# One split of V per chunk, low parts in a pool of their own, a later row load and 52 gather pairs beside the routing

## The chip, the cores and the metric

The kernel runs on one core of a Trainium2 chip. The metric is the time of one execution on the device in microseconds (us). A profiled execution gives the trace from which all rows below come.

## The reference, cut to what matters

The program is a block of attention, gated recurrence and a retrieval layer (PEER), followed by a second block of two layers. The change lies in the retrieval layer, which works on 512 tokens of width 1024 with 16384 experts, stored as two tables U and V of 16384 rows:

```python
q = (t @ wq)                        # 8 heads, two halves each
s1, i1 = top_k(s[:, :, 0], 16); s2, i2 = top_k(s[:, :, 1], 16)
cand = s1[..., :, None] + s2[..., None, :]
top, pos = top_k(cand, 16); idx = take(cidx, pos)   # 16 experts a head
g = softmax(top)
a = gelu(einsum('tpkd,td->tpk', u[idx], t))
out = einsum('tpk,tpkd->td', g * a, v[idx])
```

So each token uses 8 x 16 = 128 of the 16384 experts, with weight g times gelu of its product with a row of U, and sums rows of V.

## The kernel before, in words

**Two ways for the tokens.** The 512 tokens are four tiles of 128. Tiles 1 to 3 (384 tokens, TD) are computed densely: the product with all of U, gelu, times a weight that is zero for experts not chosen, then the product with all of V. Tile 0 goes by gathers: for each of its 128 choices an indirect DMA on POOL fetches one row of U (later of V) per token, 128 rows of 4 KB, and VectorE multiplies and sums it (`gathered`, L1142 to L1169). There are 256 such loads. They are stepped in pairs of two loads (one `next(gather)` is a pair), with a ring of five buffers and a lead of four loads.

**Stage U** (`ahead`, `rows_u`, `hidden`). Chunk e of 128 holds 128 experts. U is loaded by SP, split into a high and a low part (ACT L1349, DVE L1350) because a product is made of three products of parts, 24 matmuls a chunk. The result after gelu (L1364) is written to the DRAM tensor `Ad` from ACT's queue (L1374). Beside it the routing runs on DVE (`topk` for each tile, `spread`, which makes the dense weights `W` and writes them to the DRAM tensor `Wd`). `weave` emits three generators by virtual clocks: the chunks of U at 2.66 each, the routing by the values that it yields, and the gather pairs at GATHER[phase] each, where the phase is the number of the routing's turn. Turn 0 is `topk` of tile 0, turn 1 `topk` of tile 1, turns 2 and 3 are a `topk` and a `spread`, turn 4 is the last `spread`. Summed from the code, one `topk` yields 47.6 and one `spread` 46.4. The pairs that didn't fit stay for stage V as `gather_left`, out of 130.

**Stage V** (L1047 to L1083). For each chunk `operands` loads the 384 gelu values back (`act`, SP, L1384) and 512 KB of V (`w`, SP, L1386), multiplies `act` with the weights `Wr` (DVE, L1390), splits V and the product into `vh`, `vl`, `sh`, `sl` (ACT L1391 and L1392, DVE L1393 and L1394), in two of eight chunks has no load of weights and in the other six loads a sixth of the next group's `Wr` (SP, L1406), and at its end splits V a second time by `split` (ACT L134, DVE L136) under the same tile names. The operands that `products` takes are those of the second split. `products` makes 18 matmuls of 512 columns a chunk, four chunks behind (OPS_LAG). The order on PE, DVE and ACT is the order written in this loop. The gather pairs that are left are spread evenly over the first 120 chunks.

**Memory around it.** Pools are a stack from the left and one from the right. `h2`, the moving rows of U (32 KB of a partition), is the first on the right and is shut after U's last chunk. Then `pm` opens on the right and holds all operands of V. A tile waits only for the tiles that lay on its bytes. On the left `ar` opens where `pa` (the `act` tiles of stage U) lay, for one row of gates `gt2r`, loaded by SP (L371) and used after V (L1096). After V, `pt` opens on the right where the operands lay.

Of the kernel before, what the change touches and what calls it, by code (L numbers as in the profile page):

```python
# [8 lines left out]
FR = mybir.dt.float32r  # L9
# [13 lines left out]
TD = S - T0  # L23
# [5 lines left out]
VBUFS = 6  # L29
# [2 lines left out]
WT = 16  # L32
GBUFS = 5
GAHEAD = 4
GATHER = (13.0, 13.0, 9.0, 6.0, 4.5)
OPS_LAG = 4
TAIL = 2
STATE = 3.0
# [14 lines left out]
def run(gen):  # L53
    while True:
        try:
            next(gen)
        except StopIteration as e:
            return e.value


def steps(gen, n):
    for _ in range(n):
        yield next(gen)


def weave(*gens):

    at = [[0.0, i, g] for i, g in enumerate(gens)]
    while at:
        cur = min(at, key=lambda x: (x[0], x[1]))  # L70
        try:
            cur[0] += next(cur[2])
        except StopIteration:
            at.remove(cur)
# [18 lines left out]
class Net:  # L93
# [931 lines left out]
    def peer(self):  # L1025
        nc, p = self.nc, self.p
        hh, hl = self.h2
        mv = ([hh[:, k] for k in range(KC)], [hl[:, k] for k in range(KC)])
        first = self.proj_first(self.ws, mv, lambda i: self.normed_half(i, [(hh, hl, self.a2)], 1e-6, self.sh2))
        self.finish = None  # L1030
        for name in ("wo", "st", "hca", "y", "pn"):
            self.shut(name)
        mk = self.pool("mk")
        self.mk = mk.tile([128, 2, 2, C], F32, name="mk")
        self.mv = mk.tile([128, 2, 2, C], F32, name="mv")
        self.open_stream()
        self.Wd = self.tc.dram_tile([TD // WT, 128, 128, WT], F32, name="Wd")
        self.Ad = self.tc.dram_tile([128, 128, TD], F32, name="Ad")
        pg = self.pool("pg")
        self.rows_natural(pg)  # L1040
        sc = self.queries(mv, first)
        pq = self.pool("pq", "right")
        pa = self.pool("pa")
        dense = tuple([x[:, T0:] for x in part] for part in mv)
        ahead = self.ahead(pa, dense)
        self.chosen = None
        gather = self.gathered(pg)  # L1047
        with self.tc.manual_schedule(engines={mybir.EngineType.PE}):
            weave(self.route(pq, pg, sc), steps(ahead, 128 - REST), self.until_routed(gather))
        self.shut("pq")  # L1050
        self.shut("psc")
        run(ahead)
        self.shut("pa")
        self.shut("h2")
        pm = self.pool("pm", "right")
        ar = self.pool("ar")
        for i in range(GROUP - WLATE):
            self.spread_rows(pm, 0, i)
        rows = self.rows_of(3, "gt2r", ar)
        banks = [[self.bank() for _ in range(2)] for _ in range(3)]  # L1060
        ops = {}
        held = []
        left = self.gather_left
        done = 0
        E = mybir.EngineType
        with self.tc.manual_schedule(engines={E.PE, E.DVE, E.Activation}):
            for e in range(128 + OPS_LAG):
                if e < 128:
                    ops[e] = self.operands(pm, e)
                want = left * min(e + 1, 120) // 120  # L1070
                for _ in range(done, want):
                    next(gather, None)
                done = max(done, want)
                if e >= OPS_LAG:
                    x = e - OPS_LAG
                    if x < 128 - TAIL:
                        self.products(banks, range(3), [(x, ops.pop(x))])
                    else:
                        held.append((x, ops.pop(x)))
        run(gather)  # L1080
        for t in range(3):
            self.products(banks, [t], held)
        self.shut("pm")  # L1083
        pt = self.xp = self.pool("pt", "right")
        nf = pt.tile([128, D], F32, name="nf")
        nc.scalar.dma_start(nf, self.rowb(p['normf'], D))
        self.ss = ss = self.sp.tile([128, 4, 2], F32, name="ssx")
        self.xh = {}
        self.ws = [self.first_weights(p['awin'], 2304, q) for q in range(2)]
        for t in range(4):  # L1090
            sq = self.sp.tile([128, 2], F32, name="ssp")
            for h in range(2):
                b = banks[t - 1][h] if t else self.accg[:, h * 512:(h + 1) * 512]
                hs = slice(h * 512, (h + 1) * 512)
                y = pt.tile([128, 512], F32, name="y2", bufs=2)
                nc.vector.tensor_tensor(out=y, in0=b, in1=rows[:, hs], op=OP.mult)  # L1096
                nc.vector.tensor_tensor(out=self.X[:, t, hs], in0=self.X[:, t, hs], in1=y, op=OP.add)
                self.square_sum(self.X[:, t, hs], sq[:, h:h + 1], pt.tile([128, 512], F32, name="sqx", bufs=2))
            r = self.rstd(sq, 1e-6)
            for h in range(2):  # L1100
                hs = slice(h * 512, (h + 1) * 512)
                nc.vector.scalar_tensor_tensor(self.X[:, t, hs], self.X[:, t, hs], r, nf[:, hs], op0=OP.mult, op1=OP.mult)
                self.square_sum(self.X[:, t, hs], ss[:, t, h:h + 1], pt.tile([128, 512], F32, name="sqx", bufs=2))
            self.unit(t, 1e-5, 4)
        self.shut("ar")
        self.shut("pg")
# [23 lines left out]
    def gathered(self, pg):  # L1130
# [20 lines left out]
        for n in range(len(jobs) + GAHEAD):  # L1151
# [18 lines left out]
            if n % 2:  # L1170
                yield GATHER[self.phase]

# [204 lines left out]
    def operands(self, pm, e):  # L1377

        nc, p = self.nc, self.p
        n, j = divmod(e, GROUP)  # L1380
        if j == 0:
            self.Wr = self.Wn
        a = pm.tile([128, TD], F32, name="act", bufs=ABUFS)
        nc.sync.dma_start(a, self.Ad[e])  # L1384
        v = self.st.tile([128, 2, 512], F32, name="w", bufs=WBUFS)
        nc.sync.dma_start(v.rearrange("p a b -> p (a b)"), p['V'][e])  # L1386
        vh, vl = (pm.tile([128, 2, 512], FR, name=n, bufs=VBUFS) for n in ("vh", "vl"))
        sh, sl = (pm.tile([128, TD], FR, name=n, bufs=VBUFS) for n in ("sh", "sl"))
        a3 = a.rearrange("p (b t) -> p b t", t=WT)
        self.anchor = nc.vector.tensor_tensor(out=a3, in0=a3, in1=self.Wr[:, :, e % GROUP], op=OP.mult)  # L1390
        nc.scalar.activation(vh, v, AF.Copy)  # L1391
        nc.scalar.activation(sh, a, AF.Copy)  # L1392
        nc.vector.tensor_tensor(out=vl, in0=v, in1=vh, op=OP.subtract)  # L1393
        nc.vector.tensor_tensor(out=sl, in0=a, in1=sh, op=OP.subtract)  # L1394
        if j >= WLATE and e < 128 - GROUP:
            self.spread_rows(pm, n + 1, j - WLATE)
        vh, vl = self.split(pm, v, [128, 2, 512], "v", bufs=TAIL + OPS_LAG)
        return sh, sl, vh, vl

    def spread_rows(self, pm, n, i):  # L1400
# [460 lines left out]
```

## Time and profile before

| what | us |
|---|---|
| median of 3 runs (lowest to highest) | 3129.43 (3128.04 to 3133.86) |
| the profiled execution's own time | 3129.33 |
| its span in the trace | 3127.5 |
| PE busy | 2937.5 (94%) |
| DVE busy | 2033.6 (65%) |
| ACT busy | 1387.3 (44%) |
| POOL busy | 458.0 (15%) |
| DMA moved | 544.63 MB, mean 174 GB/s |

The shares are means over stages with different limits: stage U lies at about 662 to 1338 us of the span, stage V at about 1350 to 1987 us. Outside of the span lie 1.8 us. A busy PE is not a PE at its peak, since matmuls are pipelined and one that waits for its operands can count as busy.

### The profile page before, as it was taken

To read this page: it belongs to the slowest core of one execution; us is meant where nothing else is said; L and a number is where in the kernel's file an instruction comes from. 1 tells how busy PE (TensorE), PEld (TensorE's weight loads), DVE (VectorE), ACT (ScalarE), POOL (GpSimd) and SP (SyncE) were. 2 spreads that over 40 slices of the span, in tenths; PEclk is the share of its full clock that TensorE was granted. 3 is DMA by queue.
4 is the path that set the end of the run, shared out by engine and by line. 5 is a ranking of instruction groups with operands and counts; after the bars stand their busy time and mean duration, and the time that the engine had idled before them with its cause. 6 is when DMAs were issued, how large, how long until landed. Compare 5 with 4: busy or idle time off the path is not lost.

```text
span 3127.5 us, 42558 instructions
## 1 busy us (share of the span) xinstructions
PE 2937.5 (94%) x16010; PEld 2488.1 (80%) x16010; DVE 2033.6 (65%) x3768; ACT 1387.3 (44%) x2404; POOL 458.0 (15%) x399
## 2 busy tenths in 40 slices
PE   7898998999999999978888888899999999999998
PEld 5787987899998999966666666678888887788887
DVE  5744496459999867679999999644433335543323
ACT  4233563343466667844444444533322234433222
POOL 2100000000111222224444443000000000000000
PEclk9999999999999999999999999899999999999999
DMA  6622202345666778899999998222333222123332
GB/s 251 226 69 78 62 1 95 108 133 193 225 231 218 267 263 290 294 311 337 342 338 337 341 341 306 87 71 90 101 99 97 95 88 66 51 88 96 100 102 81
DMA packets 262510, 544.63 MB, mean 174 GB/s; under 512 B 21904, under 2 KB 139936, under 8 KB 257952
## 3 DMA queue, kind: packets, MB, share of 16 engines
q1 hardware_dynamic: 200096, 350.28, 34.1%
q0 software_dynamic: 36896, 134.25, 12.6%
q10 hardware_dynamic: 25312, 57.39, 5.0%
q8 instruction: 125, 2.05, 0.3%
q14 instruction: 81, 0.66, 0.1%
HBM read 489.38 MB, written 52.45 MB: 173 GB/s over the span
## 4 chain that ended last, share of the span: by engine, by line
PE 53%; DVE 23%; issue 10%; DMA 2%; POOL 1%; ACT 1%; SPq 0%; POOLq 0%; ACTq 0%; DVEq 0%
PE bank L123 51%; DVE vl L1393 4%; DVE accg L1166 3%; DVE gr L1161 3%; DVE act L1390 2%; DVE sl L1394 2%; DVE wl L1350 1%; POOL gr L1142 1%; PE bank L608 1%; PE bank L1500 1%; DVE A L826 1%; DVE KX L802 1%; DVE QX L803 0%; DMA gr<-in_Un_dram,iu 0%; DVE tmp L1240 0%
## 5 line engine op out<-in xcount | busy, mean ns | idle before, releaser
L123 PE MATMUL bank<-hh,wl 128*128 128x512 f32 (+2 forms) x2304 | 837.0, 364 | 31.7 <-DVE wl L1350 21.2
L123 PE MATMUL bank<-hh,wh 128*128 128x512 f32 (+2 forms) x2304 | 840.5, 366 | 10.8 <-ACT wh L149 4.4
L123 PE MATMUL bank<-hl,wh 128*128 128x512 f32 (+2 forms) x2304 | 834.8, 362 | 1.8 <-DVE hl L273 1.1
L150 DVE TENSOR_TENSOR wl<-w,wh 128x1024 fp32r<-128x1024 f32 (+2 forms) x280 | 295.2, 1055 | 645.9 <-ACT wh L149 639.0
L149 ACT ACTIVATE wh<-w 128x1024 fp32r<-128x1024 f32 (+2 forms) x280 | 257.4, 920 | 746.1 <-PE bank L123 602.9
L123 PEld LDWEIGHTS bank<-hh,wl 128*128 128x128 f32 x2304 | 437.8, 190 | 89.9 <-DVE wl L1350 32.3
L123 PEld LDWEIGHTS bank<-hh,wh 128*128 128x128 f32 x2304 | 436.7, 190 | 64.8 <-ACT wh L149 5.0
L123 PEld LDWEIGHTS bank<-hl,wh 128*128 128x128 f32 x2304 | 437.8, 190 | 49.2 <-DVE hl L273 1.9
L1142 POOL DMA_INDIRECT gr<-in_V_dram,iv x128 | 212.4, 1660 | 588.1 <-DVE gr L1161 546.2
L123 PE MATMUL bank<-vl,sh 128*128 128x512 f32 x768 | 247.7, 404 | 42.9 <-DVE vl L136 42.8
L123 PE MATMUL bank<-vh,sh 128*128 128x512 f32 x768 | 245.4, 401 | 36.9 <-ACT vh L134 36.9
L123 PE MATMUL bank<-vh,sl 128*128 128x512 f32 x768 | 237.9, 391 | 0.0
L123 PEld LDWEIGHTS bank<-vl,sh 128*128 128x128 f32 x768 | 137.6, 188 | 105.7 <-DVE vl L136 82.0
L123 PEld LDWEIGHTS bank<-vh,sh 128*128 128x128 f32 x768 | 139.6, 188 | 89.8 <-ACT vh L134 63.5
L1142 POOL DMA_INDIRECT gr<-in_Un_dram,iu x128 | 165.9, 1296 | 295.1 <-DVE gr L1161 158.3
L1392 ACT ACTIVATE sh<-act 128x384 fp32r<-128x384 f32 x128 | 67.3, 526 | 309.1 <-DVE act L1390 309.1
L1349 ACT ACTIVATE wh<-w 128x1024 fp32r<-128x1024 f32 x128 | 135.4, 1058 | 142.3 <-PE bank L123 133.4
L1350 DVE TENSOR_TENSOR wl<-w,wh 128x1024 fp32r<-128x1024 f32 x128 | 156.1, 1220 | 62.1 <-ACT wh L1349 62.1
L123 PEld LDWEIGHTS bank<-vh,sl 128*128 128x128 f32 x768 | 144.5, 188 | 31.3
L217 POOL TENSOR_TENSOR r<-r,mhalf 128x1 f32<-128x1 f32 x37 | 21.7, 590 | 987.2 <-DVE r L216 979.8
L1161 DVE SCALAR_TENSOR_TENSOR gr<-gr,h 128x1024 f32<-128x1024 f32 x128 | 155.9, 1219 | 15.4 <-DMA gr<-in_Un_dram,iu 15.4
L1166 DVE SCALAR_TENSOR_TENSOR accg<-gr,wt,accg 128x1024 f32<-128x1024 f32 x127 | 162.7, 1281 | 0.4
(369 smaller groups left out, 5059.2 us busy)
## 6 DMA issues: line engine op xcount, KB each, us to landing
w<-in_U_dram SPq DMA_DIRECT2D x128, 512.0 KB
w<-in_V_dram SPq DMA_DIRECT2D x128, 512.0 KB
w<-in_wgu_dram SPq DMA_DIRECT2D x84, 512.0 KB
Ad<-act ACTq DMA_DIRECT2D x128, 192.0 KB
Wd<-W ACTq DMA_DIRECT2D x24, 1024.0 KB
Wr<-Wd SPq DMA_DIRECT2D x96, 256.0 KB
act<-Ad SPq DMA_DIRECT2D x128, 192.0 KB
w<-in_wdown_dram SPq DMA_DIRECT2D x44, 512.0 KB
```

Source lines behind the costliest of these rows:

```text
L123: return self.nc.tensor.matmul(out, a, b, start=start, stop=stop)
L149: self.nc.scalar.activation(hi[:, :, :n], w[:, :, :n], AF.Copy)
L150: (self.low or self.nc.vector).tensor_tensor(out=lo[:, :, :n], in0=w[:, :, :n], in1=hi[:, :, :n], op=OP.subtract)
L1142: nc.gpsimd.indirect_dma_start(out=t, out_offset=None, in_=table, in_offset=bass.IndirectOffsetOnAxis(ap=idx, axis=0))
L1161: nc.vector.scalar_tensor_tensor(t, t, 1.0, self.h0, op0=OP.mult, op1=OP.mult, accum_out=dots[:, h, k:k + 1])
L1166: nc.vector.scalar_tensor_tensor(acc, t, wt[:, h, k:k + 1], acc, op0=OP.mult, op1=OP.add)
L1349: nc.scalar.activation(uh, w, AF.Copy)
L1350: nc.vector.tensor_tensor(out=ul, in0=w, in1=uh, op=OP.subtract)
L1390: self.anchor = nc.vector.tensor_tensor(out=a3, in0=a3, in1=self.Wr[:, :, e % GROUP], op=OP.mult)
L1392: nc.scalar.activation(sh, a, AF.Copy)
L1393: nc.vector.tensor_tensor(out=vl, in0=v, in1=vh, op=OP.subtract)
L1394: nc.vector.tensor_tensor(out=sl, in0=a, in1=sh, op=OP.subtract)
```

## The change

Five edits. The second split at the end of `operands` goes. `vl` and `sl` move to a new pool `pl`, opened ahead of `pm` on the right, that is on the bytes of `h2`; `vh`, `sh`, `act` and `Wr` stay in `pm`, which so lies on the bytes of the routing's pools. The pool `ar` and the load of `gt2r` move from ahead of the loop over chunks to behind its last gather. The paces of the gather pairs in turns 3 and 4 fall from 6.0 and 4.5 to 4.4 and 2.8. `pl` is shut with `pm`.

```diff
-GATHER = (13.0, 13.0, 9.0, 6.0, 4.5)
+GATHER = (13.0, 13.0, 9.0, 4.4, 2.8)
@@ peer
         self.shut("h2")
+        self.late = self.pool("pl", "right")
         pm = self.pool("pm", "right")
-        ar = self.pool("ar")
         for i in range(GROUP - WLATE):
             self.spread_rows(pm, 0, i)
-        rows = self.rows_of(3, "gt2r", ar)
@@
         run(gather)
+        ar = self.pool("ar")
+        rows = self.rows_of(3, "gt2r", ar)
         for t in range(3):
             self.products(banks, [t], held)
-        self.shut("pm")
+        for name in ("pm", "pl"):
+            self.shut(name)
@@ operands
-        vh, vl = (pm.tile([128, 2, 512], FR, name=n, bufs=VBUFS) for n in ("vh", "vl"))
-        sh, sl = (pm.tile([128, TD], FR, name=n, bufs=VBUFS) for n in ("sh", "sl"))
+        vh, vl = (x.tile([128, 2, 512], FR, name=n, bufs=VBUFS) for x, n in ((pm, "vh"), (self.late, "vl")))
+        sh, sl = (x.tile([128, TD], FR, name=n, bufs=VBUFS) for x, n in ((pm, "sh"), (self.late, "sl")))
@@
             self.spread_rows(pm, n + 1, j - WLATE)
-        vh, vl = self.split(pm, v, [128, 2, 512], "v", bufs=TAIL + OPS_LAG)
         return sh, sl, vh, vl
```

## Rows read from the trace of the kernel before

**Rows 1.** Windows by stage: length, busy us by engine (instructions), granted clock, DMA share, GB/s.
```profile
662.00:1338.00 676.00, 652.37 (x3995) 638.75 (x3994) 561.25 (x1438) 409.17 (x768) 117.89 (x82) 0.99 0.71 240
1260.00:1300.00 40.00, 38.38 (x245) 37.16 (x245) 32.05 (x44) 32.83 (x69) 11.12 (x8) 1.00 0.85 295
1338.00:1350.00 12.00, 0.70 (x4) 0.38 (x3) 2.36 (x4) 3.20 (x5) 0.00 (x0) 0.74 0.82 258
1350.00:1954.00 604.00, 536.06 (x2162) 394.86 (x2162) 602.02 (x749) 292.71 (x367) 260.71 (x175) 1.00 0.97 335
```

**Rows 2.** Waits in 1400 to 1880 us: who for whom, total us, times, longest.
```profile
PE bank L123 <- DVE vl L136: 34.2, 72, 0.5
```

**Rows 3.** The chain of waits in stage V: start us, us, what (x merged).
```profile
1368.17 0.47 DVE act L1390
...
1371.32 0.55 DVE act L1390
...
1373.46 1.10 issue
1374.56 1.23 DVE gr L1161 x2
...
1376.99 0.47 DVE act L1390
```

**Rows 4.** Groups by line, whole span: busy us, mean ns of one.
```profile
L136 DVE TENSOR_TENSOR vl<-w,vh 128x1024 fp32r<-128x1024 f32 x128 | 156.9, 1226 | 0.0
L134 ACT ACTIVATE vh<-w 128x1024 fp32r<-128x1024 f32 x128 | 133.8, 1045 | 0.0
```

**Rows 5.** The chain of waits at the end of stage V.
```profile
1954.55 32.04 PE bank L123 x140
```

**Rows 6.** DMA queues (SP's, then the gathers') in 1400 to 1880 us: packets, MB, share.
```profile
q1 hardware_dynamic: 65440, 87.57, 52.4%
q0 software_dynamic: 20736, 75.51, 45.4%
```

**Rows 7.** Windows of 1 us in stage V, columns as in the first group.
```profile
1400.00:1401.00 1.00, 0.73 (x3) 0.63 (x4) 1.00 (x2) 0.00 (x0) 0.00 (x0) 1.00 1.03 405
1418.00:1419.00 1.00, 1.00 (x6) 0.84 (x5) 1.00 (x3) 1.00 (x2) 0.94 (x1) 1.00 0.69 135
1879.00:1880.00 1.00, 1.00 (x6) 0.81 (x6) 1.00 (x2) 1.00 (x2) 0.69 (x2) 1.00 1.07 373
```

**Rows 8.** Timeline from U to V: start us, us, engine, line.
```profile
1332.77 4.53 SPq L1406 DMA_DIRECT2D Wr<-Wd  x6
...
1338.12 0.34 PE L123 MATMUL bank<-hh,wl 128*128 128x384 f32 x1
...
1342.83 0.33 SPq L371 DMA_DIRECT2D gt2r<-Rd  x1
1343.26 1.33 SPq L1384 DMA_DIRECT2D act<-Ad  x3
...
1347.64 0.56 DVE L1390 TENSOR_TENSOR act<-act,Wr 128x384 f32<-128x384 f32 x1 [15.32 <-DMA act<-Ad]
...
1348.23 0.52 ACT L1392 ACTIVATE sh<-act 128x384 fp32r<-128x384 f32 x1 [8.31 <-DVE act L1390]
...
1349.76 1.22 PE L123 MATMUL bank<-vh,sh 128*128 128x512 f32 x2 [11.30 <-ACT vh L134]
```

**Rows 9.** Waits of SP's queue in 1330 to 1352 us, columns as in the second group.
```profile
SPq L371 <- DMA Ad<-act: 5.5, 1, 5.5
```

**Rows 10.** Line L1142 in 1400 to 1880 us: from issue to landing.
```profile
DMA to landing us min/median/max: 5.2/7.0/8.4
```

**Rows 11.** Line L1142 in 600 to 1340 us: durations in ns, first and last start.
```profile
L1142 POOL DMA_INDIRECT gr<-in_Un_dram,iu x49: 937/1346/1892, 750.9 to 1313.1; - x49
L1142 POOL DMA_INDIRECT gr<-in_V_dram,iv x32: 935/1742/3783, 887.3 to 1311.1; - x32
```

**Rows 12.** Start of the three turns that spread, columns as in the group above.
```profile
L1311 DVE COPY eT<-bank x3: 410/418/418, 845.7 to 1217.0; 128x256 f32<-128x256 f32 x3
```

**Rows 13.** Timeline at the end of stage V.
```profile
1985.25 0.34 ACTq L1086 DMA_DIRECT2D nf<-in_normf_dram  x1
```

## The prediction

> **What bounds the kernel now.** Read the windows by stage first [rows 1]. In stage V, from 1350 to 1954 us, VectorE is busy 602.02 of 604 us, while PE counts 536 and moves at a full granted clock; the DMA share is 0.97. So V is bound by VectorE, with DMA just behind it. The waits say the same: PE waits for the low part of the second split, 72 times in 480 us [rows 2], and the chain of waits runs through VectorE alone [rows 3] until 1954.55 us, where the last gathers are done and PE takes over for 32.04 us [rows 5]. In stage U it is the other way round: PE is busy 652 of 676 us and VectorE 561, over its last third about 32 of 40 us with a DMA share of 0.85 [rows 1]. Between the stages PE stands idle for about 11 us [rows 8].
>
> **V: VectorE.** The chain gives the period of a chunk as the distance of two starts of its first step [rows 3]: 3.15 us without a gather pair (1368.17 to 1371.32), and a pair takes 2.43 us more (1374.56 to 1376.99). 130 pairs less the 40 that the first 81 loads make [rows 11] leave 90, spread over 120 chunks: 0.75 x 2.43 + about 3.17 = 5.0 us a chunk. The change removes the second subtraction, 1.23 us long [rows 4] but worth 1.10 us in the chain (the stretch that it calls issue [rows 3]; neighbours overlap a little). Left for V are 130 - 52 = 78 pairs, 0.65 a chunk. VectorE then needs 3.17 - 1.10 + 0.65 x 2.43 = 3.65 us a chunk. The ACT copy that goes with it (1.05 us [rows 4]) is off the path: ACT was busy 293 of 604 us [rows 1].
>
> **V: what is late next.** Two limits lie above 3.65. PE without waits makes 140 matmuls in 32.04 us [rows 5], 0.2289 us each, so 18 cost 4.12 us a chunk. DMA: in 480 us, that is 96 chunks, SP's queue moved 87.57 MB and the gathers 75.51 MB [rows 6]. That is 0.912 MB a chunk and, for 144 loads of 0.524 MB, the rest. After the change a chunk asks for 0.912 + 1.3 x 0.524 = 1.593 MB. What DMA can give is the one unknown that matters, since no stretch of the trace shows it as the only bound. Bounds: 340 GB/s, the mean over these 480 us (163.08 MB), is surely reached, and gives 1.593 / 0.340 = 4.69 us. That mean contains stretches in which nothing was asked for, as 1418 us with 135 GB/s, while other microseconds carry 405 GB/s [rows 7], which would give 3.93 us, less than PE needs. I take the mean over those of the 480 windows of 1 us whose share is 0.97 or more; there are 339, the first and the last of them stand in [rows 7], and they carry 374.5 GB/s. They contain the loads of weights with their short pieces too, so this is the rate of this mixture when DMA is asked without pause. It gives 4.25 us a chunk, just above PE's 4.12.
>
> So V after is 120 x 4.25 + 8 x 4.12 (the last chunks have no gathers) + 2 us to fill = 545 us. Before, V ran from 1349.76 [rows 8] to 1986.59 [rows 5], 636.8 us. **Term: -91.8 us**, with ends -109.4 (PE alone, 527.4 us) and -39.6 (DMA at 340 GB/s, 597.2 us).
>
> **A page against the change.** In the 1 us windows the core moves 405 GB/s with gathers and loads mixed [rows 7]. The Trainium skill, DMA: Bandwidth & Descriptors, section Where 436 GB/s comes from, says that transfers between HBM and SBUF are bound by HBM at about 358 GB/s per core. By an estimate from that figure a chunk would take 4.45 us and V 569 us, and the kernel would end near 3061 us instead of 3037. By that rule no microsecond of 405 should be seen while it holds; the row speaks against it as a hard bound.
>
> **From U to V.** SP issues the six weight loads until 1337.30 us, then the row load `gt2r` at 1342.83 and only behind it the first `act` [rows 8]. It waited 5.5 us for U's last write to leave the `act` tile under it [rows 9], and every load of V is queued behind it. The first step on VectorE starts 4.38 us after the first `act` load is issued, and PE 2.12 us later, since the operand that PE takes is the second split [rows 8]. After the change `act` can follow the weights at 1337.3, its tile now lies on the routing's bytes, and lands by about 1341.7 at the same 4.38 us. PE then waits for the product and `sh` only, 1.11 us (1347.64 to the end of `sh` at 1348.75), and starts near 1342.8 to 1343.3 instead of 1349.76. **Term: -6.5 us**; ends -9 (loads land sooner) and -3 (the weights land later, since `Wd` is written later). The low parts wait for U's last matmul, which is over by then: nothing.
>
> **U: twelve more pairs.** From the yields, turn 3 lasts 94 and turn 4 46.4 in virtual time: 94/6 + 46.4/4.5 = 15.7 + 10.3 pairs before, 94/4.4 + 46.4/2.8 = 21.4 + 16.6 after, 12 more, and 40 before agrees with the 81 loads [rows 11]. In turn 3 VectorE has room. Turn 4 starts at 1217 us [rows 12] and ends about 105 us later; its 6.3 new pairs cost 15.3 us of VectorE, which was busy 32.05 of 40 us there [rows 1], so 0.80 + 0.15 = 0.95, and 6.6 MB, 63 GB/s on top of 295 [rows 1], below the 374.5 of above. Queued behind a pair on VectorE are the low part of U's next chunk and the masks of `spread`, and PE waits for both. So it nearly fits; some pairs will make PE wait. Cost between 0 and 12 x 2.43 = 29 us (all exposed). I take **+6 us**, nearer to the first end, since most of the room is there.
>
> **The end.** `gt2r` is now queued on SP behind the last V load and ahead of the second block's weights. Those loads are issued while PE still works off its last chunks for 32 us [rows 5], so the row is hidden; if PE were the bound to the end, it would still land before. The load of `nf` was issued 1.3 us ahead of V's end [rows 13], and now lies on tiles that PE reads late: 0, ends -1 and +2.
>
> **Sum.** Against the profiled execution's own time, 3129.3 (0.1 us off the median): 3129.3 - 91.8 - 6.5 + 6 + 0 = **3037.0 us**.
>
> **Rivals.** (1) PE bounds V: DMA gives over 387 GB/s when asked, as the best microseconds do [rows 7], and chunks take 4.12 us. 3129.3 - 107.4 - 6.5 + 3 = 3018; floor near 3011. Against it: the loads of weights never ran at that rate. (2) DMA is the wall already: its share of 0.97 [rows 1] is all there is, and the holes come back because SP waits for buffers in order. 4.69 us a chunk: 3129.3 - 39.6 - 5 + 8 = 3093. Against it: gathers land in 7.0 us at the median [rows 10], well within the lead of four loads. (3) The second subtraction goes but something as long takes its place on VectorE, a wait for a buffer or a gathered row; then only the 12 pairs count, 120 x 0.1 x 2.43 = 29 us: 3129.3 - 29 - 6.5 + 6 = 3100. (4) Slower: the ring of gathers becomes the bound. Five buffers return after landing plus about 3 us for POOL's issue and VectorE, so a chunk takes at least 1.3 x (L + 3) / 5. With L = 7.0 [rows 10] that is 2.6 us; if a saturated DMA lets L rise, it decides from about 16 us on, where it gives the old 5.0 us a chunk and VectorE stands in order behind the missing row. At L = 18 a chunk takes 5.46 us, V 690 us, the kernel 3182 us. The longest landing shown is 8.4 us [rows 10].
>
> **How the numbers follow.** Forecast (3025 to 3052) 0.47; rival 1 (3011 to 3025) 0.27; rival 2 (3052 to 3095) 0.19; rival 3 0.03; rival 4 0.04. The range 3011 to 3076 leaves out the last two and part of rival 2, in sum under 0.2. A measurement of this kernel tells about 0.2% (6 us) from no change. Faster by more: 0.95; within: 0.01; slower: 0.04.
>
> **What would show it.** In the trace after, line L136 should be gone from V and VectorE busy below 0.9 of the stage, at about 4.25 us for eight-chunk means. With DMA as the bound its share stays at 1.0 or above without holes and PE waits for operands whose releaser is a DMA; under rival 1 PE has no idle and holes remain. V should start 5 us after U's last matmul, with `act` right behind the weights on SP. 104 or 105 gather loads should lie ahead of V, and the end of U a few us later than 1338, with PE waits for VectorE after about 1220 us. Wrong would be: a V of over 600 us, gathered rows as the releaser of VectorE with landings over 12 us, or a U longer by over 15 us.

## The result and the profile after

The changed kernel takes 3026.45 us (median; 3022.93 to 3031.0), the kernel before 3130.91 beside it: a ratio of 0.9667, 95% interval 0.9649 to 0.9685. Forecast were 3037.0 us, 3011 to 3076. The profiled execution took 3022.93 us, span 3021.1; it is the quickest of its four, so sums over stages stand against it, not against the median.

Stages, from the two traces (the first ACT copy of U, U's last matmul, V's first and last matmul, the end of the span):

| us | before | after | change | forecast |
|---|---|---|---|---|
| ahead of stage U | 662.8 | 665.8 | +3.0 | 0 |
| stage U | 675.7 | 681.3 | +5.6 | +6 |
| gap from U to V | 11.3 | 2.8 | -8.5 | -6.5 |
| stage V | 637.3 | 538.8 | -98.5 | -91.8 |
| behind V's last matmul | 1140.5 | 1132.5 | -8.0 | 0 |
| span | 3127.5 | 3021.1 | -106.4 | -92.3 |

The page after: busy us and share of the span, and GB/s in 40 slices.

```profile
PE 2908.7 (96%) x16010; PEld 2499.0 (83%) x16010; DVE 1886.9 (62%) x3640; ACT 1267.4 (42%) x2276; POOL 448.6 (15%) x399
...
GB/s 250 242 66 81 64 8 71 119 119 145 220 232 219 227 317 302 329 357 385 376 382 383 384 384 269 43 98 91 96 93 98 98 88 60 43 98 98 98 99 83
```

Windows of stage V and of the last third of stage U after, columns as in [rows 1].

```profile
1370.00:1829.00 459.00, 455.90 (x1972) 364.38 (x1971) 395.04 (x541) 164.09 (x222) 206.90 (x142) 1.00 1.05 381
1260.00:1300.00 40.00, 38.22 (x248) 36.95 (x247) 37.16 (x51) 34.24 (x74) 19.67 (x14) 1.00 0.97 357
```

Against [rows 1], VectorE in V falls from 602 of 604 us to 395 of 459 (0.86), PE is busy nearly throughout, and DMA stands at a share of 1.05 and 381 GB/s, not only in single microseconds. The waits in V name it. (Columns as in [rows 2], 1370 to 1830 us.)

```profile
ACT vh L1393 <- DMA w<-in_V_dram: 129.6, 47, 6.7
...
DVE vl L1395 <- ACT vh L1393: 62.3, 27, 6.1
...
PEld bank L123 <- ACT sh L1394: 9.9, 21, 1.5
```

Where PE waited for VectorE's second split [rows 2], ACT now waits for rows of V to land, VectorE for ACT, and little of it reaches PE. In the whole view no row has VectorE waiting for a gathered row. Both queues, columns as in [rows 6], in 1370 to 1830 us:

```profile
q1 hardware_dynamic: 74647, 100.53, 62.2%
q0 software_dynamic: 20433, 74.42, 42.1%
```

That is 0.93 MB a chunk of V by SP (100.53 in 108 loads of V) and gathers beside it, as the forecast summed. 105 gathers lie ahead of V instead of 81 [rows 11]. The transition, as in [rows 8]:

```profile
1331.62 10.47 SPq L1407 DMA_DIRECT2D Wr<-Wd  x6
...
1342.19 2.12 SPq L1386 DMA_DIRECT2D act<-Ad  x3
...
1346.76 0.34 PE L123 MATMUL bank<-hh,wl 128*128 128x384 f32 x1
...
1349.87 1.22 PE L123 MATMUL bank<-vh,sh 128*128 128x512 f32 x2 [2.78 <-ACT sh L1394]
```

The first `act` is issued right behind the weights, 4.9 us ahead of the end of U's last matmul, where before it was issued 4.8 us behind it [rows 8].

### The profile page after: what moved, and what is told of

Same layout as the page of the kernel before. It is cut to its first block, busy times and chain, and to the rows that moved or that the text cites. A ratio compares the mean times of both kernels' runs of the same rounds, so it can differ in the third digit from the quotient of the medians.

```text
span 3021.1 us, 42371 instructions
## 1 busy us (share of the span) xinstructions
PE 2908.7 (96%) x16010; PEld 2499.0 (83%) x16010; DVE 1886.9 (62%) x3640; ACT 1267.4 (42%) x2276; POOL 448.6 (15%) x399
## 3 DMA queue, kind: packets, MB, share of 16 engines
q0 software_dynamic: 36896, 134.25, 12.1%
## 4 chain that ended last, share of the span: by engine, by line
PE 55%; DVE 13%; DMA 10%; issue 8%; ACT 2%; POOL 1%; SPq 1%; ACTq 0%; POOLq 0%; DVEq 0%
PE bank L123 53%; DMA w<-in_V_dram 6%; DMA Wr<-Wd 2%; DVE accg L1168 2%; DVE wl L1352 1%; DMA act<-Ad 1%; DVE vl L1395 1%; DVE sl L1396 1%; PE bank L608 1%; DMA gr<-in_Un_dram,iu 1%; DVE gr L1163 1%; PE bank L1501 1%; POOL gr L1144 1%; DVE act L1392 1%; DVE A L826 0%
## 5 line engine op out<-in xcount | busy, mean ns | idle before, releaser
L123 PE MATMUL bank<-hh,wh 128*128 128x512 f32 (+2 forms) x2304 | 844.1, 367 | 11.2 <-ACT wh L149 4.8
L1144 POOL DMA_INDIRECT gr<-in_V_dram,iv x128 | 202.4, 1581 | 449.7 <-DVE gr L1163 409.6
L123 PE MATMUL bank<-vl,sh 128*128 128x512 f32 x768 | 239.7, 393 | 0.9
L1395 DVE TENSOR_TENSOR vl<-w,vh 128x1024 fp32r<-128x1024 f32 x128 | 156.1, 1220 | 67.7 <-ACT vh L1393 67.6
L1393 ACT ACTIVATE vh<-w 128x1024 fp32r<-128x1024 f32 x128 | 134.8, 1053 | 145.7 <-DMA w<-in_V_dram 141.5
```

The lines of the kernel that those rows point to most:

```text
L123: return self.nc.tensor.matmul(out, a, b, start=start, stop=stop)
L1144: nc.gpsimd.indirect_dma_start(out=t, out_offset=None, in_=table, in_offset=bass.IndirectOffsetOnAxis(ap=idx, axis=0))
```

## The experiments

All by the same stages. A ratio is to the kernel before, with its interval; the two without one ran once.

| kernel | us | ratio | U | gap | V | behind V |
|---|---|---|---|---|---|---|
| after, again | 3023.24 | 0.9649 [0.9625, 0.9672] | 683.1 | 1.9 | 538.2 | 1132.5 |
| split_once | 3067.4 | 0.9789 [0.9771, 0.9808] | 677.5 | 10.7 | 574.8 | 1140.0 |
| old_paces | 3049.22 | 0.9731 [0.9715, 0.9748] | 678.2 | 0.4 | 574.7 | 1133.6 |
| row_early | 3022.65 | 0.9651 [0.9634, 0.9667] | 679.9 | 1.1 | 539.1 | 1133.0 |
| one_pool | 3033.41 | 0.9682 [0.9662, 0.9701] | 679.5 | 6.5 | 541.5 | 1139.8 |
| before_no_loads | 3132.26 | | 675.4 | 12.1 | 637.1 | 1143.1 |
| after_no_loads | 3010.41 | | 680.4 | 0.3 | 523.1 | 1138.2 |
| more_pairs | 3017.52 | 0.9632 [0.9616, 0.9648] | 695.4 | -0.1 | 523.6 | 1132.8 |
| spread_127 | 3016.04 | 0.963 [0.9607, 0.9654] | 681.3 | 2.4 | 532.8 | 1133.3 |
| spread_127_56 | 3022.39 | 0.9656 [0.9637, 0.9674] | 701.3 | 0.6 | 522.8 | 1132.4 |
| one_pool_y_left | 3031.45 | 0.9686 [0.967, 0.9703] | 679.5 | 6.4 | 540.2 | 1137.8 |

The changed kernel was run again (3014.4 to 3028.7 us). Expected was:

> The changed kernel again, on the chip of the next three. Near 3026.

**What bound V before.** In the kernel before, the pairs of stage V load nothing, and VectorE works on a row that is there:

```diff
         def load(key, table, idx):
+            if not self.routing:
+                ring[key] = None
+                return
             ring[key] = t = pg.tile([128, D], F32, name="gr", bufs=GBUFS)
@@
                 t = ring.pop(n - GAHEAD)
+                src = self.h0 if t is None else t
+                if t is None and what == "u":
+                    t = pg.tile([128, D], F32, name="gr", bufs=GBUFS)
```

(`src` then stands for `t` as the first operand of the two steps on VectorE.)

> The kernel before, but the gather pairs of stage V load nothing: VectorE does the same multiplications on a row that is there (so the sums of tile 0 are not the reference's), DMA moves 0.79 MB a chunk less. Theory (VectorE alone bounds V before): V stays at 637 us within 5, the kernel near 3130. Rival B (DMA at a share of 0.97 shares the bound): V falls by 20 us or more.

Stage V took 637.1 us, with and without the loads, while DMA fell to this (window, columns as in [rows 1]):

```profile
1370.00:1927.00 557.00, 494.14 (x1999) 364.07 (x1998) 555.44 (x696) 270.48 (x339) 0.00 (x0) 1.00 0.61 184
```

VectorE was the bound; the 0.97 of DMA in [rows 1] cost nothing. Rival B fell.

**The split alone.** The kernel before without its last line of `operands`:

```diff
-        vh, vl = self.split(pm, v, [128, 2, 512], "v", bufs=TAIL + OPS_LAG)
```

> The kernel before without its second split of V, all else as it was (40 pairs beside the routing, one pool, the row load early). Theory (VectorE bound V before; once it is relieved, V goes at the rate of DMA when it is asked without pause, 383 GB/s in the trace after, or of PE, whichever is later): a chunk asks 0.912 + 1.5 x 0.524 = 1.698 MB, 4.43 us, V = 120 x 4.43 + 8 x 4.12 + 2 = 567 us instead of 637, the gap from U to V about 1 us shorter, the kernel near 3060. Rival A (PE bounds V, the full DMA queues are an accident): V 530 to 534, kernel near 3026, so all of the gain. Rival B (DMA was the wall at 340 GB/s already): V stays near 637, kernel near 3130.

**The paces alone.** The changed kernel with its old paces:

```diff
-GATHER = (13.0, 13.0, 9.0, 4.4, 2.8)
+GATHER = (13.0, 13.0, 9.0, 6.0, 4.5)
```

> The kernel after with the old paces of the gather pairs (6.0 and 4.5), so 40 pairs beside the routing instead of 52. Theory (DMA rate): V 567 us instead of 533, stage U about 4 us shorter, the kernel about 30 us slower than the changed one, near 3056. Rival A (PE bounds V): V stays at 533, U 4 us shorter, the kernel near 3022, faster than the changed one.

V took 574.8 and 574.7 us, with one pool and with two, at these rates (the split alone, then the old paces):

```profile
1372.00:1867.00 495.00, 471.89 (x1977) 368.03 (x1976) 422.63 (x574) 164.71 (x223) 232.83 (x164) 0.98 1.03 375
```

```profile
1364.00:1858.00 494.00, 468.98 (x1963) 363.75 (x1962) 422.11 (x574) 164.68 (x223) 234.39 (x164) 0.98 1.04 377
```

So the split alone is worth 62.5 us of V and the twelve pairs another 36. Twelve pairs are 29 us of work on VectorE, which was idle for 72 us of that window: they don't pay there but in DMA. 1.698 MB a chunk at 376 GB/s are 4.52 us, and 120 x 4.52 + 8 x 4.09 + 2 = 577; the rate is that of the same windows, so this sum only shows that the terms are complete. Rival A fell in both.

Both V's lie 8 us above the 567 that I expected, which took 383 GB/s for the rate. The windows of 1 us with a share of 0.97 or more do carry 384 GB/s in both; the mean loses it in between. Some of these holes go with a lower granted clock after a wait of PE: in 1732 to 1736 us of `split_once` it is 0.57, and DMA moves 300 GB/s. How much of the 8 us that makes, no run shows.

**V's floor.** The same omission in the changed kernel (the diff of above):

> The kernel after with the same part left out: no loads for the pairs of stage V, the same work on VectorE. Theory: DMA asks 0.912 MB a chunk only, PE is the bound alone, 128 x 4.12 = 527 us, V 528 to 530 instead of 533: the pairs that are left cost 3 to 5 us. Rival A (V has other stalls, for VectorE in order): V stays at 533.

and more pairs beside the routing, with V as it was:

```diff
-GATHER = (13.0, 13.0, 9.0, 4.4, 2.8)
+GATHER = (13.0, 13.0, 9.0, 3.7, 2.2)
```

> The kernel after with paces 3.7 and 2.2, some 60 pairs beside the routing. Theory: a chunk of V asks 0.912 + 1.17 x 0.524 = 1.52 MB, 3.98 us at 383 GB/s, under PE's 4.12, so V falls by at most 4 us to 529; U grows, since VectorE is at 0.9 and DMA near 357 GB/s in its last third already: 3 to 15 us. The kernel is 0 to 11 us slower than the changed one. Rival A (V is bound by PE in the changed kernel already): V stays, the kernel is slower by all that U grows.

Both take V to 523.1 and 523.6 us, and PE is never idle (no loads, then more pairs, where the second row is the last turn of the routing):

```profile
1367.00:1804.00 437.00, 437.00 (x1929) 361.97 (x1929) 401.56 (x548) 169.32 (x225) 0.00 (x0) 1.00 0.74 234
```

```profile
1381.00:1822.00 441.00, 441.00 (x1947) 365.19 (x1946) 377.73 (x516) 164.61 (x222) 187.56 (x128) 1.00 1.05 379
1231.00:1341.00 110.00, 101.84 (x634) 97.88 (x633) 103.92 (x143) 87.07 (x188) 54.21 (x40) 0.98 0.96 355
```

The floor is 523 us, and what is left of the gathers in the changed kernel costs V 15.7 us, not the 3 to 5 that I expected: I had put the floor 5 to 7 us too high (below) and the changed kernel's V at 533 us, where its trace has 538.8. For the same reasons V fell by 15.2 us in `more_pairs`, not by 4 at most, and its rival A fell. `more_pairs` pays 14.1 us in U for it; its last turn has VectorE at 103.92 of 110 us and PE idle for 8. Its interval overlaps that of the changed kernel's repeat and just misses that of the first measurement (0.9649 to 0.9685), so a gain isn't shown. The stretch behind V is 2.6 and 5.7 us longer in the two kernels without loads, but behind PE's very last matmul (11.7 and 13.6 us to the end of the span instead of 8.7), not at the end of V.

**The rate asked.** The left pairs spread over 127 chunks instead of 120, so that a chunk asks less and V as much in all. A second kernel has this and pace 3.8 in turn 3 (instead of 4.4), so some 55 pairs beside the routing:

```diff
-                want = left * min(e + 1, 120) // 120
+                want = left * min(e + 1, 127) // 127
```

> The kernel after with its left gather pairs spread over 127 chunks of V instead of 120. Theory (V pays for what a chunk asks of DMA over 381 GB/s): 78/127 pairs a chunk ask 0.912 + 1.23 x 0.524 = 1.556 MB, 4.08 us, just PE's own pace, so V falls from 539 to 525 to 529 us and the kernel to near 3015. Rival (the 16 us over PE's floor come from VectorE's order or from the start of V, not from the rate asked): V stays within 3 us of 539.

> As the one before and pace 3.8 in turn 3, so some 55 pairs beside the routing. Theory: 0.912 + 1.175 x 0.524 = 1.528 MB, 4.01 us, below PE's pace; V at its floor, 523 to 525 us; turn 3 grows by 1 to 3 us. Kernel 3013 to 3016. Rival: the third turn's pairs cost PE their full 2.43 us each, and the kernel is 8 us above the one before.

The first took V from 538.5 (mean of the changed kernel and its repeat) to 532.8, a fall of 5.7 us where I expected 10 to 14. The mechanism has the right sign, but its time and that of the repeat overlap in their intervals. Of the 10 us over the floor that are left, 8.7 lie in two places of its trace. At chunks 37 and 45 PE loses 4.3 us, where ACT stood 6.9 and 6.8 us for a late load of V. At V's end it loses 4.4 us: VectorE takes two gathered rows and a split of the next block's first weights between the operands of the last two chunks, PE waits 2.5 us for the last `sh`, and its granted clock is 0.58 in the 4 us behind that. The rate asked on the mean is only part of what V pays.

The second has V at its floor and loses it in U: turns 2 and 3 together took 392.9 us, where they take 373.4 to 378.6 in the other kernels with 52 pairs, for three more pairs. Its waits (VectorE in 1060 to 1360 us; PE in 1000 to 1230 us):

```profile
DVE gr L1163 <- DMA gr<-in_Un_dram,iu: 32.2, 9, 7.8
...
PE bank L123 <- DVE wl L1352: 21.5, 8, 7.5
```

VectorE stands in order behind gathered rows that are late, the low part of U's next chunk stands behind them, and PE waits for it. In the repeat of the changed kernel these are 15.8 and 11.2 us. The kernel is 6.4 us above the one before, near the rival's 8, but by another sum: U alone grew by 20 us, 6.7 a pair instead of 2.43, and V gave 10 back. The count of pairs doesn't set this price: `more_pairs` has a faster pace still in turn 3 (3.7), and its waits are 22.6 and 12.3 us. Why the rows were so late here stays open.

**The place of the row load.**

```diff
         pm = self.pool("pm", "right")
+        ar = self.pool("ar")
         for i in range(GROUP - WLATE):
             self.spread_rows(pm, 0, i)
+        rows = self.rows_of(3, "gt2r", ar)
@@
         run(gather)
-        ar = self.pool("ar")
-        rows = self.rows_of(3, "gt2r", ar)
```

> The kernel after with the pool ar and the load of gt2r back ahead of V. Theory: SP waits for U's last write before it issues the first act, so PE starts V 5 to 8 us later than after the change; V runs at a DMA rate from its first chunk, so nothing catches up, and the kernel is 5 to 8 us slower than the changed one, near 3033. Rival: the queues fill while PE waits and V makes good for it, or the load of weights is late anyway, as late as act: under 2 us.

My theory fell: gap 1.1 us, the same time. SP's queue, in its order of time:

```profile
1337.39 1.61 SPq L1386 DMA_DIRECT2D act<-Ad  x3
...
1351.44 0.32 SPq L371 DMA_DIRECT2D gt2r<-Rd  x1
```

SP's order isn't among those written by hand; the framework plans it. With two pools the first `act` is free to go ahead, and the plan has it 14 us before the row though the row stands first in the code. In the changed kernel, where the row stands last, it goes at 1366.7 us, among the first loads of V.

**The pool of the low parts.**

```diff
-        self.late = self.pool("pl", "right")
-        pm = self.pool("pm", "right")
+        pm = self.late = self.pool("pm", "right")
@@
-        for name in ("pm", "pl"):
-            self.shut(name)
+        self.shut("pm")
```

> The kernel after with vl and sl back in pm, so that pm begins on the bytes of U's moving rows again. Theory: the first tiles of pm wait for U's last matmul, the first act or weights are issued at U's end and land some 4 us later, the gap from U to V is 6 to 8 us instead of 2.8, the kernel 3 to 5 us slower than the changed one, near 3030. Rival: what lies on these bytes is not loaded first, as the weights of before were issued ahead of U's end: no difference over 1 us.

The gap is 6.5 us as expected: SP issues the first `act` 2.6 us after U's last matmul. With one pool and the row early it was 10.7 (`split_once`, which also has the old paces), so there the row's place is worth some 4 us. But another 7 us went where I hadn't looked, behind V. The first rows show SP at the gap and VectorE at V's end with one pool:

```profile
1348.07 1.28 SPq L1384 DMA_DIRECT2D act<-Ad  x3
```

```profile
1893.20 0.69 DVE L1096 TENSOR_TENSOR y<-accg,gt2r 128x512 f32<-128x512 f32 x1 [14.09 <-PE bank L123]
```

Tile 0's sum needs nothing of PE, yet its second half waits 14.1 us for PE: its tile `y` must lie on bytes of an operand that PE reads to the end. All of VectorE's work behind V queues behind it. After the change both halves run ahead of V's end:

```profile
L1098 DVE TENSOR_TENSOR y<-accg,gt2r x2: 684/688/691, 1880.1 to 1880.7; 128x512 f32<-128x512 f32 x2
```

So I moved `y` alone off those bytes:

```diff
-                y = pt.tile([128, 512], F32, name="y2", bufs=2)
+                y = ar.tile([128, 512], F32, name="y2", bufs=2)
```

> The kernel with one pool for V's operands as in one_pool, but the tile y of the sum after V lies on the left, in ar. Theory (the 7 us by which the stretch after V is longer with one pool come from y, which lies on an operand that PE reads last, so that VectorE waits in order): the stretch from V's last matmul to the end falls from 1139.8 to 1132 to 1134 us, the kernel from 3033 to near 3026. Rival (another tile of that pool or the load of nf): no change.

Only 2 of the 7 us came back. The wait of `y` was gone, and the next tiles of the same pool took its place, the load of `nf` and ACT's `sqx`, after V's last matmul at 1891.92 us or just ahead of it:

```profile
1891.50 0.34 ACTq L1086 DMA_DIRECT2D nf<-in_normf_dram  x1
1891.89 0.63 ACT L207 ACTIVATE sqx<-X 128x512 f32<-128x512 f32 x1 [12.08 <-PE bank L123]
```

So it is the pool `pt` on late operands, not one tile of it; that moving the pool's place does it, `one_pool` against the changed kernel shows (1139.8 and 1132.5 us).

## Why the prediction was right, and where it was off

**V, right in mechanism.** Step one, VectorE as the only bound before, is shown by `before_no_loads`. Step two, DMA at its saturated rate just above PE as what is late next, is shown by `split_once` and `old_paces`: at the higher demand V goes by bytes, 575 us. For the changed kernel itself `after_no_loads` shows it: without the loads V is 15.7 us shorter. The rate taken from the saturated microseconds [rows 7], 374.5 GB/s, came out as 375 to 381 over whole stages. But DMA is the bound only in part of V: means over eight chunks of PE's starts lie between 4.1 us, which is PE's own pace, and 4.37, not at 4.25 throughout. Rivals 3 and 4 fell, as VectorE waits for no gathered row in V. Open is how much of what is left is the rate of DMA and how much SP's waiting for a buffer of `w`, which VectorE frees (93.1 us in 44 waits, in 1370 to 1829 us): no run has more buffers.

**The term that was mis-sized.** -91.8 came out as -98.5. The chunks took 4.21 us on the mean (538.8 / 128) instead of 4.25. DMA moved 381 GB/s, which by the forecast's sum gives 4.18 us a chunk and 536 us. PE's price was wrong too; it hardly counts in that sum, but it sets the floor. I divided 32.04 us by 140 matmuls [rows 5], and that stretch also holds a first step of 0.33 us and the end of its last matmul. In `after_no_loads` V's 18 x 128 = 2304 matmuls take 523.1 us, 0.2270 each, 4.09 us a chunk. So rival 1's floor of 527 was 4 us too high, and the changed kernel lies between forecast and rival 1.

**The figure of 358 GB/s.** 381 GB/s for 459 us in one piece speak against it as a bound on this core alone, in the place of the Trainium skill that the prediction names (DMA: Bandwidth & Descriptors, Where 436 GB/s comes from). The 3061 us that the prediction estimated from it weren't seen.

**From U to V.** -8.5 for -6.5, within the ends of -9 and -3. The cause was half wrong: the sum gave the gain to the row load and took the pool as what lets `act` follow the weights. The runs give it to the pool; with it the row's place is worth nothing, without it about 4 us. The row doesn't wait for the last V load either, as the prediction had it: it goes 17 us after V's start.

**U.** +5.6 for +6. With 40 pairs U took 677.5 and 678.2 us in two kernels and 675.7 before, with 52 pairs 679.5 to 683.1. So the pairs cost 1 to 6 us against the two and 4 to 7 against before, and equal U code differs by some 3 us between executions: that the term hits to 0.4 us is chance. VectorE rose from 32.05 [rows 1] to 37.16 of 40 us, 0.93 for the 0.95 forecast. That the pairs fit only just is shown by 55 and 60 pairs, with 20 and 14 us more. The 3.0 us ahead of U are no effect of the change: nothing is changed there, and U's first copy lies between 662.0 and 668.0 us in these kernels.

**The end: the step that failed.** I put it at 0, -1 to +2, having looked at `nf` alone [rows 13]. It gave -8.0. In the trace of before the wait was to be seen: the chain leaves PE at 1986.59 us [rows 5] for VectorE's sum of tile 0, which no bank of PE feeds.

```profile
1986.61 0.69 DVE L1096 TENSOR_TENSOR y<-accg,gt2r 128x512 f32<-128x512 f32 x1 [6.59 <-PE bank L123]
```

This second half of the sum starts 0.4 us ahead of the end of V's last matmul; after the change it starts 7.9 us ahead of it. The new pool should put `pt` on `vl` and `sl`, and the part of it that is written first comes free before V's last matmul; which bytes these are follows from the order of the pools, no view shows it.

## What to carry to other kernels

When the bound engine is relieved, take the next limit from the stretches in which that queue is never empty, not from its mean: here 374.5 against 340 GB/s decided 52 us of forecast, and the saturated rate held over the whole stage. A pool that moves changes two waits, that of the tiles laid on it and that of the tiles laid on it next; look up both ends, and ask of a wait which bytes it is for when no data runs that way. Work moved beside another stage pays in the queue that is full, not only on the engine that runs it: the same twelve pairs were worth 36 us of DMA in V and cost 1 to 6 in U, and a few more cost 14 to 20.

## What the runs showed that was not expected

DMA moved 381 GB/s over 459 us with gathers and loads mixed, at a share of 1.05 by the profile, so a share of 0.97 was not the limit; without gathers the same V loads ran at 234 GB/s and PE never waited. A load's place in the code needn't be its place in SP's queue: the row load went behind the first `act` in both places.
